# A streaming-encoder layer: the second product's weight loads on another queue, the order of its last products, and the spacing of the attention's softmax blocks

## The chip, the cores and the metric

The kernel runs on one core of a Trainium2 chip, as one program. The metric is the device time of one execution in microseconds (us). The engines are TensorE (PE, with its weight loads as PEld), VectorE (DVE), ScalarE (ACT), GpSimd (POOL) and SyncE (SP, which here only asks for transfers); 16 DMA engines move the data.

## The reference

One pre-norm layer for 1024 positions of width 1024 in float32: a mixing part of three branches with gates, then a SwiGLU feed-forward part, then a final RMSNorm.

```python
proj = rms_norm(x, norm_mix_g) @ w_in          # split into the branches' inputs
o_conv = conv_module(...)                      # GLU, causal depthwise conv of width 31, LayerNorm, SiLU, pointwise product
o_gla = gla(...)                               # 4 heads, chunks of 64
# differential attention: 8 heads, two components of 64, key chunks of 64 up to the query's chunk
s = einsum('bqhtd,bkhtd->bhtqk', q_block, k) * scale
p = softmax(where(mask, s, -inf))
pd = p[:, :, 0] - lam * p[:, :, 1]
o = einsum('bhqk,bkhv->bqhv', pd, v)           # then an RMSNorm
y = sigmoid(m_conv) * o_conv + sigmoid(m_gla) * o_gla + sigmoid(m_diff) * o_diff
x = x + y @ w_out
gate, up = split(rms_norm(x, norm_ffn_g) @ w_ffn_in, 2)   # 2816 each
x = x + (silu(gate) * up) @ w_ffn_out
return rms_norm(x, final_norm_g)
```

## The kernel before

Precision. Every product of float32 matrices is made of three matmuls: the operands are split into a rounded part and the rest (`hilo`: a copy on ACT, L125, and a subtraction on DVE, L126), and `mm3` (L132 to L134) multiplies the parts. A matmul on 512 columns starts 0.23 us after the one before it, where nothing holds it up.

Order. A matmul stream of projections is the main line. Beside it, generators of other work (`spawn`) are stepped by `tick`, a few times in each product; a step of that kind is called a part here. How many ticks lie between a generator's steps is what it yields. The Tile framework adds the waits and may move instructions a little; each engine then executes its list in order, and so does the queue of transfers that SP asks for.

Attention. `diff_core(h)` handles the eight query blocks of one head. Block `qb` has n = 128 (qb + 1) keys. `softmax` multiplies both components' scores (L729, L730), masks the last 64 keys of the upper rows, takes the row maxima (L733 for one component when n is above 512, L736 for both otherwise), and lets ACT take the exponentials (L739). Up to n = 512 both components share one tile of two PSUM banks (`sc`); from the fifth block on (n = 640) each component has a tile of its own. There are two such tiles at a time. `turn` transposes the result, `values` multiplies by the values. The plan (L783 to L785) puts block i's `softmax` at part `at`, its `turn` at `at + LAG[i]` and its `values` three parts after that, and `at` then grows by `SPACE[i]`. While this runs, PE multiplies projections, and DVE also carries the steps of the depthwise convolution (L448). When the cores are done, `conv_norm` and `conv_split` make the operand `u` of the pointwise product.

SwiGLU. Both products are done in Strassen's manner with seven products per group (Winograd's form). The weight operands of the second product are made beforehand from sums, stored to DRAM (`wt_d`, by `right_units`), and loaded back as tiles `tt` of 1 MB by `load_t` (L1288 to L1296), asked for on SP's queue; a ring of 14 tiles is used, so that a load waits until the last product that reads the tile 14 places before it is done. The gated products of the first half are stored to `m_d` (L1231) and come back through `load_mid` (L1324). `load_x3` (L1301) loads the rows that the result is added to.

The last stage goes through 16 `ROUNDS` (t, j0, j1), and each round n through the products p = 0 to 6. The list `order2` (L1349 to L1352) is the order in which the products of two neighbouring rounds alternate. A product adds to one of three chains: `"abacaab"[p]` says which. Chains a and b are the two halves of one two-bank tile `sc`, chain c is a bank `pb`. After each product but the first, DVE adds the chain to the rows x (L1344); the chain's tile is written on by the next product of that chain. In the rounds that finish a row block, `final` takes its square sum on ACT (L1410, L1414), a small step on DVE (L1415), the power -1/2 on POOL (L1416), and the scaling on DVE (L1419); then the result is stored (L1421).

In before, `order2` ends with (15,0), (14,4), (15,1), (15,2), (14,5), (14,6), (15,3), (15,4), (15,6), (15,5). Products of round 14 or 15 have two `k` blocks, six matmuls on 512 columns.

Of the kernel before, what the change touches and what calls it, by code (L numbers as in the profile page):

```python
# [63 lines left out]
AHEAD = 7  # L64

MIX0, MIX1 = 2, 18
LAG = (3, 3, 3, 3, 4, 4, 4, 4)
SPACE = (2, 2, 2, 2, 2, 2, 3, 3)
TAP_RATE = {"head": 0.0, "blocks": 0.45, "gla": 0.45, "diff": 0.82}


def body(nc, tc, I, out):
    x_d, w_d, wf_d, wfup_d, par_d, lq_d, cst_d, msk_d, ffg_d, fng_d = I
    vec, act, pe, pool, sp = nc.vector, nc.scalar, nc.tensor, nc.gpsimd, nc.sync
# [33 lines left out]
    wt_d = dram.tile([(7 * FT // 2 + 1) // 2, P, 4, HALF], F32, name="wt_d")  # L108
# [9 lines left out]
    def f(ap):  # L118
        return ap.bitcast(F32)
# [588 lines left out]
    def diff_core(h):  # L708
# [74 lines left out]
        for i in range(NT):  # L783
            plan += [(at, first, i), (at + LAG[i], second, i), (at + LAG[i] + 3, third, i)]
            at += SPACE[i]  # L785
        now = 0
# [471 lines left out]
    def right_units():  # L1258
        for j in range(PAIRS):
            raw = keep.tile([P, 2, S], F32, tag="kb", name="wo")  # L1260
            for c in range(2):
                sp.dma_start(raw[:, c, :], w_d[first + NU + j, c])
            yield 4
            b11, b12, b21, b22 = (raw[:, c, hs(half)] for c in range(2) for half in range(2))
            ts = fbs[0].tile([P, HALF], F32, tag="ts", name="ts", bufs=1)
            src = (b11, b12, b12, b21, ts, b12, b22)
            for p in range(7):
                if p == 1:
                    vec.tensor_tensor(out=ts, in0=b22, in1=b12, op=ALU.subtract)
                    vec.tensor_tensor(out=b12, in0=b12, in1=b11, op=ALU.subtract)  # L1270
                elif p == 2:
                    vec.tensor_tensor(out=b12, in0=b22, in1=b12, op=ALU.subtract)
                elif p == 5:
                    vec.tensor_tensor(out=b12, in0=b21, in1=b12, op=ALU.subtract)
                u = 7 * j + p
                if u % 2 == 0:
                    to = keep.tile([P, 4, HALF], F32R, tag="kb", name="to")
                hilo(to[:, u % 2 * 2, :], to[:, u % 2 * 2 + 1, :], src[p])
                if u % 2 or u == 7 * PAIRS - 1:
                    n = u % 2 * 2 + 2  # L1280
                    sp.dma_start(wt_d[u // 2][:, 0:n, :], f(to[:, 0:n, :]))
                yield 2
        for i in range(2):
            load_t(i)

    RING = 14
    tt, x3 = {}, {}

    def load_t(i):
        if i >= NTL:  # L1290
            return
        at = i % RING
        pool_, tag = (keep, "kb") if at in (0, 1, 6, 7) else (big, "big") if at < 12 else (fcs["fc"], "tt")
        tt[i] = pool_.tile([P, 4, HALF], F32R, tag=tag, name="tt", bufs=8 if at < 12 else 2)
        n = 2 if i == NTL - 1 and 7 * PAIRS % 2 else 4
        sp.dma_start(f(tt[i][:, 0:n, :]), wt_d[i][:, 0:n, :])  # L1296

    def load_x3(t):
        x = keep.tile([P, 2, D], F32, tag="kb", name="x3")
# [48 lines left out]
    NR = len(ROUNDS)  # L1348
    order2 = [(0, p) for p in range(4)]  # L1349
    for n in range(NR - 1):  # L1350
        order2 += [(n + 1, 0), (n, 4), (n + 1, 1), (n + 1, 2), (n, 5), (n, 6), (n + 1, 3)]
    order2 += [(NR - 1, p) for p in (4, 6, 5)]  # L1352
    makes2 = [(n, p) for n in range(NR) for p in range(7)]
    last_use = {}
    for at, (n, p) in enumerate(order2):
# [11 lines left out]
    for at, (n, p) in enumerate(order):  # L1367
        if at == 4:
            drain()
            tail.release()  # L1370
            fbs.append(tc.alloc_tile_pool(name="fb", bufs=1))
            spawn(t4_block(), 7)
        for _ in range(2 if at > 4 else 1):
            if len(fb.made) < (4 if at < 12 else AHEAD):
                fb.make()
        fb.product(n, p)
        if at == 14:
            spawn(right_units(), 0)
        if n == NU - 1:
            for i in {0: (2, 3), 1: (4, 5), 2: (6, 7), 3: (8, 9), 6: (10, 11)}.get(p, ()):  # L1380
                load_t(i)
            if p == 4:
                load_x3(0)
        if at == len(order) - 12:
            load_mid(0)
        if fb.nxt == len(order):
            load_mid(1)
        if fb.nxt == len(order) and f2.nxt < 7 and len(fb.made) + len(f2.made) < AHEAD:
            f2.make()
        fb.after(n, p)  # L1390
# [32 lines left out]
    for at, (n, p) in enumerate(order2):  # L1423
        for _ in range(2):
            if len(f2.made) < AHEAD:
                f2.make()
        if p == 0 and n in (1, 2):
            load_x3(n + 1)
        if (n, p) == (2, 0):
            for i in (12, 13):  # L1430
                load_t(i)
        if (n, p) == (4, 0):
            sp.dma_start(fng, fng_d)
            act.activation(fng, fng, AF.Copy, scale=ROOT)
        f2.product(n, p)
        f2.after(n, p)
        for i in loads.get(at, ()):
            load_t(i)
# [59 lines left out]
def _program(arrays):  # L1498
    import concourse.bacc as bacc

    nc = bacc.Bacc("TRN2", target_bir_lowering=False, num_devices=1, dynamic_dma_scratch_size=1024)
    ins = [nc.dram_tensor(n, v.shape, mybir.dt.from_np(v.dtype), kind="ExternalInput").ap() for n, v in arrays.items()]
    out = nc.dram_tensor("out_0_dram", (NT, P, D), F32, kind="ExternalOutput").ap()
    with tile.TileContext(nc) as tc:
        body(nc, tc, ins, out)
    return nc
# [9 lines left out]
```

## Time and profile before

| what | value |
| --- | --- |
| median of three runs | 2047.68 us (2047.64 to 2050.73) |
| the profiled execution | 2049.43 us |
| its span | 2047.7 us |
| its granted TensorE clock, mean | 0.999 |
| PE busy | 2009.8 us, 98% |
| DVE, ACT, POOL busy | 72%, 45%, 3% |
| transfers on the hardware queue q1 | 290.19 MB |
| transfers on the software queue q0 | 6.82 MB |

The span is the time from the first to the last record of the profiled execution; the execution's own time is a little longer. In the rows below, a row of a timeline has the start, the duration, the engine, the line, the operation, the tile written from the tiles read, and its form; in brackets stands how long the engine stood idle before it, and what ended that.

### The profile page before, as it was taken

The page shows a single profiled execution, that of the slowest core. Times are in us where ns is not written, and L with a number is a line of the kernel's source. Part 1 is how long each engine was busy: PE and PEld are TensorE (multiplying, and loading weights), DVE is VectorE, ACT ScalarE, POOL GpSimd, SP SyncE. Part 2 cuts the span into 40 slices and gives each one's busy share as a digit, 9 for nine tenths or more (in the row PEclk, how much of TensorE's full clock was granted, in tenths as well). Part 3 has the DMA queues.
Part 4 walks back from the last instruction along what each step waited for, and adds up shares of the span by engine and source line. Part 5 has one row for each costly group of instructions (what it writes and reads, how often), then busy time and mean ns, then how long its engine had stood idle before and what let it go on. Part 6 is the DMA issues. An engine that isn't in the chain of part 4 may idle for free.

```text
span 2047.7 us, 27244 instructions
## 1 busy us (share of the span) xinstructions
PE 2009.8 (98%) x10280; PEld 1693.7 (83%) x10280; DVE 1466.8 (72%) x2306; ACT 930.4 (45%) x1969; POOL 56.6 (3%) x64
## 2 busy tenths in 40 slices
PE   7999999999999999999999999999999999999997
PEld 6888878799999988898988888887888778877775
DVE  7997878577667788787884464459776776656566
ACT  6434434445544455555555461225544544422224
POOL 1000000000000000000000000000000000000000
PEclk9999999999999999999999999999999999999999
DMA  4232242321324443434343555323667666597652
GB/s 158 98 120 88 87 128 98 119 61 58 94 77 124 129 115 81 102 83 116 78 97 99 206 181 166 105 90 112 227 238 253 227 226 237 200 381 270 223 195 88
DMA packets 125124, 298.75 MB, mean 146 GB/s; under 512 B 11744, under 2 KB 56416, under 8 KB 115264
## 3 DMA queue, kind: packets, MB, share of 16 engines
q1 hardware_dynamic: 122256, 290.19, 42.4%
q0 software_dynamic: 2736, 6.82, 2.1%
q8 instruction: 81, 1.33, 0.3%
q14 instruction: 51, 0.42, 0.1%
HBM read 183.19 MB, written 94.90 MB: 136 GB/s over the span
## 4 chain that ended last, share of the span: by engine, by line
PE 72%; issue 13%; DVE 7%; DMA 4%; ACT 3%; POOL 1%; SPq 0%; POOLq 0%; ACTq 0%; DVEq 0%
PE sc L132 12%; PE sc L133 12%; PE sc L134 12%; PE pb L132 11%; PE pb L133 11%; PE pb L134 11%; DVE acc L448 1%; DMA wo<-w_dram 1%; PE pb L766 1%; ACT p L739 1%; DMA wr<-w_dram 1%; DMA wt_d<-to 1%; POOL rs L139 1%; DMA x<-x_d 1%; PE sc L729 1%
## 5 line engine op out<-in xcount | busy, mean ns | idle before, releaser
L448 DVE SCALAR_TENSOR_TENSOR acc<-up,par,acc 128x1024 f32<-128x1024 f32 x240 | 306.8, 1278 | 0.6
L132 PE MATMUL pb<-h,wh 128*128 128x512 f32 x704 | 281.2, 400 | 1.0 <-ACT hf L310 1.0
L134 PE MATMUL pb<-h,wl 128*128 128x512 f32 x704 | 275.9, 392 | 0.0
L133 PE MATMUL pb<-h,wh 128*128 128x512 f32 x704 | 275.6, 391 | 0.0
L125 ACT CAST wh<-wr 128x512 fp32r<-128x512 f32 (+2 forms) x271 | 160.3, 609 | 202.0 <-PE sc L133 90.5
L126 DVE TENSOR_TENSOR wl<-wr,wh 128x512 fp32r<-128x512 f32 (+2 forms) x271 | 180.0, 672 | 61.7 <-ACT wh L125 58.0
L125 ACT CAST wh<-s 128x512 fp32r<-128x512 f32 (+2 forms) x216 | 123.4, 580 | 209.3 <-PE sc L133 144.3
L134 PEld LDWEIGHTS pb<-h,wl 128*128 128x128 f32 x704 | 132.4, 188 | 28.4
L132 PEld LDWEIGHTS pb<-h,wh 128*128 128x128 f32 x704 | 132.9, 189 | 26.1 <-ACT hf L310 1.2
L133 PEld LDWEIGHTS pb<-h,wh 128*128 128x128 f32 x704 | 132.8, 189 | 23.7 <-issue 0.2
L132 PE MATMUL pb<-wh,h 128*128 128x256 f32 x512 | 148.4, 290 | 0.0
L126 DVE TENSOR_TENSOR wl<-s,wh 128x512 fp32r<-128x512 f32 (+2 forms) x216 | 135.4, 638 | 16.4 <-ACT wh L125 16.3
L134 PE MATMUL pb<-wh,h 128*128 128x256 f32 x512 | 144.8, 283 | 0.0
L133 PE MATMUL pb<-wl,h 128*128 128x256 f32 x512 | 144.7, 283 | 0.0
L132 PE MATMUL sc<-bT,wh 128*128 128x512 f32 x352 | 137.4, 391 | 0.7 <-DVE t L1223 0.7
L133 PE MATMUL sc<-bT,wh 128*128 128x512 f32 x352 | 137.0, 389 | 0.0
L134 PE MATMUL sc<-bT,wl 128*128 128x512 f32 x352 | 137.0, 389 | 0.0
L132 PE MATMUL sc<-tt,wh 128*128 128x512 f32 x264 | 106.8, 408 | 7.0 <-DVE x L1344 6.3
L133 PE MATMUL sc<-tt,wh 128*128 128x512 f32 x264 | 103.7, 393 | 0.0
L134 PE MATMUL sc<-tt,wl 128*128 128x512 f32 x264 | 103.0, 393 | 0.0
L132 PE MATMUL sc<-T,wh 128*128 128x512 f32 x256 | 100.0, 391 | 2.0 <-ACT c L986 1.4
L1344 DVE TENSOR_TENSOR x<-x,sc 128x512 f32<-128x512 f32 x80 | 54.6, 686 | 63.6 <-PE sc L134 60.0
(306 smaller groups left out, 4566.7 us busy)
## 6 DMA issues: line engine op xcount, KB each, us to landing
wr<-w_dram SPq DMA_DIRECT2D x146, 512.0 KB, 3.7
wt_d<-to SPq DMA_DIRECT2D x38, 1024.0 KB, 4.2
tt<-wt_d SPq DMA_DIRECT2D x38, 1024.0 KB, 6.1
m_d<-t SPq DMA_DIRECT2D x44, 256.0 KB, 4.2
wo<-w_dram SPq DMA_DIRECT2D x22, 512.0 KB, 5.8
k<-k SPq DMA_DIRECT2D x48, 128.0 KB, 2.8
kl<-kl SPq DMA_DIRECT2D x48, 128.0 KB, 2.4
wr<-m_d SPq DMA_DIRECT2D x12, 384.0 KB, 5.6
```

Source lines behind the costliest of these rows:

```text
L125: a = act.copy(hi, src)
L126: b = vec.tensor_tensor(out=lo, in0=src, in1=f(hi), op=ALU.subtract)
L132: pe.matmul(o, ah, bh, start=start, stop=False, skip_group_check=more)
L133: pe.matmul(o, ah, bl, start=False, stop=False, skip_group_check=more)
L134: pe.matmul(o, al, bh, start=False, stop=stop, skip_group_check=more)
L139: pool.tensor_tensor(out=dst, in0=dst, in1=mhalf[:, 0:width], op=ALU.pow)
L448: op = vec.scalar_tensor_tensor(out=acc, in0=up[:, j:j + S], scalar=w, in1=acc, op0=ALU.mult, op1=ALU.add)
L729: pe.matmul(sc[i][:, c], a["q"][i][:, t], a["k"][i][:, c], start=True, stop=False)
L739: act.activation((p0[:, 0:n], p1)[i], sc[i], AF.Exp, bias=st_[:, i:i + 1], accum_out=st_[:, 2 + i:3 + i])
L766: pe.matmul(ov[:, 0:P], parts[k // 4][:, c], a["v"][:, k, :], start=k == 0, stop=k == nk - 1)
L1344: vec.tensor_tensor(out=x, in0=x, in1=ch["bacaab"[p - 1]], op=ALU.add)
```

## The change

Three edits. The loads of `tt` are asked for by GpSimd (software queue) where SP asked for them (hardware queue). The end of `order2` becomes (15,0), (14,4), (15,1), (15,2), (14,5), (15,4), (14,6), (15,3), (15,5), (15,6). And `LAG` and `SPACE` change: the softmax blocks of a head began at parts 0, 2, 4, 6, 8, 10, 12, 15 and now begin at 0, 2, 4, 6, 9, 11, 13, 16; the transposes were at 3, 5, 7, 9, 12, 14, 16, 19 and are now at 3, 5, 7, 10, 13, 15, 17, 20, and the products with the values three parts after these.

```diff
-LAG = (3, 3, 3, 3, 4, 4, 4, 4)
-SPACE = (2, 2, 2, 2, 2, 2, 3, 3)
+LAG = (3, 3, 3, 4, 4, 4, 4, 4)
+SPACE = (2, 2, 2, 3, 2, 2, 3, 2)
...
         n = 2 if i == NTL - 1 and 7 * PAIRS % 2 else 4
-        sp.dma_start(f(tt[i][:, 0:n, :]), wt_d[i][:, 0:n, :])
+        pool.dma_start(f(tt[i][:, 0:n, :]), wt_d[i][:, 0:n, :])
...
         order2 += [(n + 1, 0), (n, 4), (n + 1, 1), (n + 1, 2), (n, 5), (n, 6), (n + 1, 3)]
-    order2 += [(NR - 1, p) for p in (4, 6, 5)]
+    order2[-2:] = [(NR - 1, 4), (NR - 2, 6), (NR - 1, 3), (NR - 1, 5), (NR - 1, 6)]
```

## Rows read from the trace of the kernel before

**Rows 1.** The page: busy time and share of each engine; chain by engine.
```profile
PE 2009.8 (98%) x10280; PEld 1693.7 (83%) x10280; DVE 1466.8 (72%) x2306; ACT 930.4 (45%) x1969; POOL 56.6 (3%) x64
...
PE 72%; issue 13%; DVE 7%; DMA 4%; ACT 3%; POOL 1%; SPq 0%; POOLq 0%; ACTq 0%; DVEq 0%
```
**Rows 2.** PE's waits: what for, us in total, times, longest.
```profile
PE sc L132 <- DVE x L1344: 6.3, 5, 1.9
PE sc L729 <- ACT p L739: 3.9, 5, 1.0
```
**Rows 3.** Timeline of PE, 805 to 815 us.
```profile
809.82 0.39 PE L133 MATMUL pb<-h,wh 128*128 128x512 f32 x1
811.20 0.44 PE L729 MATMUL sc<-k,q 128*128 128x384 f32 x1 [0.99 <-ACT p L739]
```
**Rows 4.** Timeline of DVE, 804 to 814 us.
```profile
808.44 1.22 DVE L736 TENSOR_REDUCE st<-sc 128x2 f32<-128x1024 f32 x1
```
**Rows 5.** Timeline of PE, 1826 to 1836 us.
```profile
1829.83 0.50 PE L132 MATMUL sc<-tt,wh 128*128 128x512 f32 x1 [1.95 <-DVE x L1344]
```
**Rows 6.** Chain of work that ended last in 1820 to 1836 us: start, us, what.
```profile
1817.14 11.93 DMA x<-x_d
```
**Rows 7.** Stretches: us, busy PE, PEld, DVE, ACT, POOL, clock, DMA share, GB/s.
```profile
1816.00:1827.00 11.00, 11.00 (x48) 8.62 (x47) 5.78 (x13) 2.71 (x7) 0.00 (x0) 1.00 1.02 394
1848.00:2008.00 160.00, 158.26 (x677) 124.30 (x676) 99.39 (x186) 43.25 (x92) 0.00 (x0) 1.00 0.60 211
...
1830.30:1833.70 3.40, 3.40 (x10) 2.62 (x9) 2.72 (x6) 1.80 (x4) 0.00 (x0) 0.50 0.93 329
```
**Rows 8.** Timeline of PE, 1913 to 1919 us.
```profile
1917.59 0.47 PE L132 MATMUL sc<-tt,wh 128*128 128x512 f32 x1 [1.74 <-DVE x L1344]
```
**Rows 9.** Timeline of PE, 2026 to 2040 us.
```profile
2031.67 0.50 PE L132 MATMUL sc<-tt,wh 128*128 128x512 f32 x1 [0.52 <-DVE x L1344]
...
2035.97 0.47 PE L132 MATMUL sc<-tt,wh 128*128 128x512 f32 x1 [1.29 <-DVE x L1344]
...
2038.38 0.50 PE L132 MATMUL sc<-tt,wh 128*128 128x512 f32 x1 [0.78 <-DVE x L1344]
```
**Rows 10.** Line L1296 alone: duration ns, first and last start; landing.
```profile
L1296 SPq DMA_DIRECT2D tt<-wt_d x39: 319/332/927, 1764.8 to 1985.3; - x39
...
DMA to landing us min/median/max: 4.6/6.1/13.2
```
**Rows 11.** SP's waits.
```profile
SPq L1296 <- PE sc L134: 95.6, 26, 8.9
```
**Rows 12.** Line L809 alone, an accumulating store asked for by GpSimd.
```profile
L809 POOL DMA_DIRECT2D y_d<-dgate x12: 862/878/932, 756.1 to 1042.4; - x12
```
**Rows 13.** Timeline of SP, 1964 to 1967 us.
```profile
1965.92 0.33 SPq L1296 DMA_DIRECT2D tt<-wt_d  x1
```
**Rows 14.** Timeline of PE, 1978.7 to 1979 us.
```profile
1978.80 0.39 PE L132 MATMUL sc<-tt,wh 128*128 128x512 f32 x1
```
**Rows 15.** DMA queues in 371.5 to 373.5 us: packets, MB, share.
```profile
q0 software_dynamic: 66, 0.27, 67.5%
q1 hardware_dynamic: 67, 0.27, 36.2%
```
**Rows 16.** Timeline of SP, 1804 to 1832 us.
```profile
1813.89 1.35 SPq L1296 DMA_DIRECT2D tt<-wt_d  x2
```
**Rows 17.** Timeline of DVE, 2027 to 2048 us.
```profile
2033.88 0.75 DVE L1419 SCALAR_TENSOR_TENSOR xn<-x,sm,fng 128x512 f32<-128x512 f32 x1 [0.66 <-POOL sm L1416]
...
2036.90 0.75 DVE L1419 SCALAR_TENSOR_TENSOR xn<-x,sm,fng 128x512 f32<-128x512 f32 x1 [0.66 <-POOL sm L1416]
2037.64 0.69 DVE L1344 TENSOR_TENSOR x<-x,sc 128x512 f32<-128x512 f32 x1
```
**Rows 18.** Timeline of PE, 1198 to 1210 us.
```profile
1202.73 0.39 PE L132 MATMUL pb<-u,wh 128*128 128x512 f32 x1
```
**Rows 19.** Timeline of DVE, 1196 to 1206 us.
```profile
1204.28 1.90 DVE L126 TENSOR_TENSOR u<-c,u 128x512 fp32r<-128x512 f32 x3 [1.00 <-ACT u L125]
```

## What the change does to the time, told before it was known

> **What bounds the kernel now.** I read the page's busy times first: PE is busy 98% of the span, and it carries 72% of the chain that ended last [rows 1]. So time can only go where PE stands still, where its clock is low, or behind its last matmul. The second view is the list of PE's waits [rows 2]: five waits of the second SwiGLU product's matmuls for the DVE addition at L1344, 6.3 us together, and five waits of the score product L729 for the exponential L739, 3.9 us together. The change touches the code around both. The third step is the timeline around each wait.
>
> The score waits all have one place, the fifth query block of a head (five of the eight heads). In the one shown, PE begins the 128x384 product at 811.20 us, 1.38 after the matmul before it, where 0.23 is usual; 0.99 of that is put down to L739 [rows 3]. The block has two score tiles of two banks, and there are two such buffers: its second tile has to wait for both exponentials of the fourth block, and these for the row maximum, which began only at 808.44 and took 1.22, behind the convolution's steps on DVE [rows 4].
>
> The L1344 waits have three places. At 1829.83 PE stood 1.95 us [rows 5], because the addition lacked the residual rows x, a load that took 11.93 us [rows 6] while the DMA engines were full (share 1.02); then TensorE, after standing, ran at half clock (0.50, the 1.2 GHz level) for some 3.4 us [rows 7]. At 1917.59 it stood 1.74 us [rows 8]. Three waits lie in the last rounds, 0.52, 1.29 and 0.78 us [rows 9], where one product follows another into the same two-bank tile and has to wait for the addition that reads it.
>
> **Part 1, the requests on GpSimd's queue.** It moves 39 requests from SP to POOL. It adds no work to PE, DVE or ACT. It takes from SP 39 issues of 0.33 us and 95.6 us of standing for buffers in front of them, 26 times [rows 10, 11]; both lay beside PE's work. On POOL a request of this kind cost 0.88 us where the trace has one [rows 12]; 39 of them are some 34 us on an engine that is 3% busy [rows 1]. What is queued behind a request waiting for its buffer is the next request only; the powers that POOL computes for the last norm come later than the last request at 1985.3 [rows 10]. A late request costs nothing while there is slack: one of the tightest loads is asked for at 1965.92 and its buffer first read at 1978.80, 12.9 us, against 6.1 for a median landing [rows 10, 13, 14], so even 4 us more is hidden; without that slack each late load would cost its lateness on PE.
>
> The open question is what two queues do to SP's other transfers: x, the stored products and their reloads. On one queue x, the second half of which was asked for at 1817.14 [rows 6], stands behind the stores and weight loads asked for before it, the last two of these at 1813.89 [rows 16]. Where the trace has both queues at work, they moved 66 and 67 packets in the same 2 us [rows 15], packet for packet. I apply that to the stretch from 1804 to 1830. The weight packets are the large ones, so they drain early although the small ones of SP are let in between; x is still last of all bytes, and the engines are full until it lands (1.02, 394 GB/s [rows 7]). So I take zero. Gain bound: the 1.95 us and the half clock go, 3.4 x 0.5 = 1.7, together -3.7, and with the 1.74 at 1917.59, -5.4. Loss bound: the stores and reloads slip behind weight packets that were asked for later, +2: the 1.95 us of [rows 5] a second time. Zero is nearest, since the bytes ahead of x are the same.
>
> The Trainium skill ("DMA: Bandwidth & Descriptors", section "Queues, rings and completion order") says that each DMA engine takes turns between queues, changing only at packet boundaries; the 66 and 67 packets agree. By it the sum would carry the same zero here, but the fast side could also be the weights, which is rival B.
>
> **Part 2, the last rounds.** No instruction is added or removed; the last six products change places. A product of the last round is six matmuls, 6 x 0.23 = 1.4 us. Before, (15,4), (15,6) and (15,5) stood in a row on one tile, and (14,5), (14,6) on another. After, (15,4) stands between those two, and (14,6) and (15,3) between (15,4) and (15,5); (15,6) still follows (15,5) directly. An addition takes 0.69, so two of the three waits go and one of about 0.8 stays: PE's last matmul comes 0.52 + 1.29 = 1.8 us earlier, some 2.1 with the restarts [rows 9]. But behind PE stands a chain that runs through DVE, ACT, DVE, POOL and DVE for each of the last four blocks, whose last steps (L1419) stand 3.02 us apart, with an addition of 0.69 in each period [rows 17], and DVE waits in it in order. If that chain sets the end, only an addition that moves out of one period is saved, some 0.6. I take the middle of 0.6 and 2.1, rounded: -1.4. Loss bound: none of it, 0, as no instruction joins.
>
> **Part 3, the softmax blocks.** The numbers give the fifth block one part more behind the fourth, and the sixth to eighth one part later each; the fourth's transposes too. A part is six or nine matmuls of the projection that runs beside it; the inserted one has six, 1.4 us. The longest wait is 0.99, so all five go: 3.9 us by [rows 2], and since the start came 1.15 late where 0.99 was put down, 0.16 more each, together -4.7. The maximum and the exponentials don't move with it, as they were issued before the inserted part. No instruction is added on any engine. What becomes late next: a head ends one part later; the last one passes that to the convolution's norm, and this to the first pointwise product, whose operand was ready just in time: PE took it at 1202.73, the next group of DVE's splits began at 1204.28 after 1.00 us of standing for ACT [rows 18, 19]. A part there is up to 2 us, while two convolution additions leave that stretch; I take +0.3, with 0 and +1.5 as ends. Bounds of the whole part: -5.3 (with another half us of waits in other heads) and +1.5 (no gain, and the late norm paid in full).
>
> **Sum.** 0 - 1.4 - 4.7 + 0.3 = -5.8 us. The profiled execution took 2049.43 us, its span 2047.7 and 1.7 around it; that gives 2043.6. It lay 1.75 above the median of 2047.68; on the median it is **2041.9 us**.
>
> **Rivals.** A: part 1 also clears the wait for x. For it: on one queue x stands behind weights, and off it only behind stores. Against: full engines. Time: 2041.9 - 3.7 = 2038.2. The Trainium skill (same page, section "Issuing engines are not separate DMA queues") says that requests of different engines end on the same 16 DMA engines and save only issue time; by that A could not be, and the time would be the 2041.9.
>
> B, the slower one: the reloads of the stored products lose to weight packets. Each round of the last stage needs a reload of small packets; each of its packets would wait for an 8 KB weight packet asked for later. Place: 1808 to 1990. Price: a wait like that of [rows 5] with its half clock, 1.95 + 1.7 = 3.7 us; it decides from the third one on, 11 - 5.8 = +5: 2053. Against: 39 loads in 220 us leave the engines at a share of 0.60 after 1848 [rows 7], and on one queue the reloads already stood behind whole weight loads.
>
> C: the score wait moves to the next step, since DVE's maximum is late for its own reasons and the sixth block now meets it. Part 3 then gives +0.3 and the time is 2047.68 - 1.1 = 2046.6. For it: DVE's convolution steps go on through the inserted part; against: the sixth block keeps its distance to the fifth.
>
> D: the compiler reorders the end so that part 2 doesn't do what it says: 2043.3. For it: the compiled order of the last products already differs from the written one by a matmul here and there.
>
> **How the numbers follow.** Forecast 0.47, A 0.18, B 0.12, C 0.15, D 0.08. 0.2% is 4.1 us, about what a measurement of this kernel can tell from no change; so faster begins under 2043.6. Faster: A, most of the forecast's own spread (2039.5 to 2044) and half of D: 0.60. Slower: B, 0.12. Same: 0.28. The range for 8 in 10 leaves out B and the lower half of A's spread: 2037.0 to 2048.0.
>
> **What will show it.** The waits of L729 for L739 at the fifth block gone from PE's list, with no new one at the sixth: step 3. Three waits for L1344 left instead of five, one of them in the last rounds, and PE's last matmul some 2 us nearer to the start of the last addition: step 2. Weight loads on the software queue, no DMA among PE's releasers, x landing near 1828, and the half clock still there: step 1. I am wrong if PE waits for pointwise operands near 1203, if x lands early, or if rounds 2 to 13 show new waits on reloads.

## The result: 1% slower, all of it in the last stage

The changed kernel took 2070.44 us (median of four runs, 2067.28 to 2072.73) where the kernel before took 2048.2 in the same comparison: ratio 1.0105, 95% interval 1.0088 to 1.0123. The prediction was 2041.9 us, between 2037.0 and 2048.0. The profiled execution took 2072.73 us, its span 2070.6.

From the page of the changed kernel, busy time of the engines and the queues (packets, MB, share of 16 engines):

```profile
PE 2017.9 (97%) x10280; PEld 1699.6 (82%) x10280; DVE 1465.4 (71%) x2306; ACT 927.6 (45%) x1969; POOL 81.0 (4%) x103
...
q1 hardware_dynamic: 116640, 249.82, 36.9%
q0 software_dynamic: 8352, 47.19, 7.3%
```

The matmuls are the same 10280; 40 MB moved to the software queue, as meant. PE was busy 8.1 us longer with the same matmuls, most of it at half clock: the trace has 20.4 us of half clock between 1829 and 1973 us, where the kernel before has 3.4, and half of the 17.0 us between them is 8.5. The rest of the loss is standing. Lining both traces up by the number of the matmul shows where PE fell behind (times of the changed kernel): it is 1.1 us late at 1790 us, 12.9 late at 1864, 17.3 at 1927, 22.5 at 1993, and no later after that. PE's last matmul is 21.0 us late and the end of the span 22.9, so the last rounds added 1.9.

PE's waits in the changed kernel (us in total, times, longest), to be held against [rows 2]:

```profile
PE sc L132 <- DVE x L1344: 13.1, 8, 4.7
...
PE sc L132 <- ACT pb L958: 3.1, 3, 2.4
PE pb L755 <- DVE dgate L807: 2.2, 3, 0.9
...
PE sc L729 <- DVE p L744: 0.9, 3, 0.4
```

The wait for L739 is gone (part 3 did that), the wait for L1344 doubled. The timeline of PE, cut to the largest of its stops:

```profile
1830.64 0.80 PE L132 MATMUL sc<-tt,wh 128*128 128x512 f32 x1 [4.72 <-DVE x L1344]
1837.74 0.51 PE L132 MATMUL sc<-tt,wh 128*128 128x512 f32 x1 [1.10 <-DVE x L1344]
1849.12 0.50 PE L132 MATMUL sc<-tt,wh 128*128 128x512 f32 x1 [2.39 <-ACT pb L958]
...
1875.94 0.47 PE L132 MATMUL sc<-tt,wh 128*128 128x512 f32 x1 [1.99 <-DVE x L1344]
...
1966.57 0.76 PE L132 MATMUL sc<-tt,wh 128*128 128x512 f32 x1 [3.01 <-DVE x L1344]
```

The first answers to [rows 5]: 4.72 us where there were 1.95. It again has a stretch of half clock (1.2 GHz) behind it, and so has the stop at 1966.57. Stretches of the changed kernel, columns as in [rows 7]:

```profile
1827.00:1834.00 7.00, 3.36 (x8) 2.71 (x9) 0.69 (x1) 0.71 (x2) 1.08 (x2) 0.66 1.00 355
1834.00:1848.00 14.00, 10.97 (x33) 7.47 (x32) 10.20 (x20) 3.33 (x7) 0.00 (x0) 0.80 0.97 368
...
1966.50:1969.50 3.00, 2.93 (x7) 2.38 (x8) 1.93 (x4) 0.00 (x0) 0.00 (x0) 0.50 1.02 431
```

Two things are to be explained: 1800 to 1850 us, and the single stops up to 1970.

**What DVE does at the later stops.** DVE in the changed kernel near the stop of 3.01 us; L901 is a sum of products that were stored and reloaded (`wr`, `mr`), from which a left operand is made:

```profile
1960.64 0.55 DVE L901 TENSOR_TENSOR s<-mr,s 128x384 f32<-128x384 f32 x1
1965.27 0.56 DVE L901 TENSOR_TENSOR s<-wr 128x384 f32<-128x384 f32 x1 [4.08 <-DMA wr<-m_d]
1965.75 0.68 DVE L1344 TENSOR_TENSOR x<-x,sc 128x512 f32<-128x512 f32 x1
```

And the same place of the kernel before:

```profile
1944.00 0.56 DVE L901 TENSOR_TENSOR s<-mr,s 128x384 f32<-128x384 f32 x1
1946.05 0.69 DVE L1344 TENSOR_TENSOR x<-x,sc 128x512 f32<-128x512 f32 x1 [1.49 <-PE sc L134]
...
1948.18 0.55 DVE L901 TENSOR_TENSOR s<-wr 128x384 f32<-128x384 f32 x1
```

In the changed kernel the sum waits for its reload, and the addition that PE waits for stands behind it. The compiled order shows that this is no accident of timing. DVE's instructions there, S n.1 being the first sum of round n, X n.p the addition after product p, l the low parts of operands:

```
before:  ... X8.5 l10.1 S10.6 X8.6 l10.2 X9.3 l10.3 S11.1 S11.2 X9.4 ...
changed: ... X8.5 l10.1 S10.6 S11.1 X8.6 l10.2 X9.3 l10.3 S11.2 X9.4 ...
```

S5.1, S7.1 and S11.1 had moved ahead of X2.6, X4.6 and X8.6; S9.1 and S13.1 stood so before as well, and the stop of [rows 8] is that of S9.1. In the first rounds, X1.1 and X1.2, which need the late rows x, now stood ahead of X0.5 and X0.6. None of that is in the diff. PE's products of the first rounds, a few matmuls and copies of ACT near these places, and SP's requests stand in another order too. Why is not shown; presumably the framework orders each engine's list by when it takes the operands to be ready, and takes a reload to land sooner when no weights stand before it in SP's list.

### The profile page after: what moved, and what is told of

Read it like the earlier page. It is cut to its first block, busy times and chain, and to the rows that moved or that the text cites. A ratio compares the mean times of both kernels' runs of the same rounds, so it can differ in the third digit from the quotient of the medians.

```text
span 2070.6 us, 27304 instructions
## 1 busy us (share of the span) xinstructions
PE 2017.9 (97%) x10280; PEld 1699.6 (82%) x10280; DVE 1465.4 (71%) x2306; ACT 927.6 (45%) x1969; POOL 81.0 (4%) x103
## 5 line engine op out<-in xcount | busy, mean ns | idle before, releaser
L132 PE MATMUL sc<-tt,wh 128*128 128x512 f32 x264 | 109.6, 418 | 17.8 <-DVE x L1344 13.1
L1344 DVE TENSOR_TENSOR x<-x,sc 128x512 f32<-128x512 f32 x80 | 54.7, 685 | 75.8 <-PE sc L134 63.4
L133 PE MATMUL sc<-tt,wh 128*128 128x512 f32 x264 | 106.7, 404 | 0.0
```

What stands on the lines that cost most here:

```text
L132: pe.matmul(o, ah, bh, start=start, stop=False, skip_group_check=more)
L133: pe.matmul(o, ah, bl, start=False, stop=False, skip_group_check=more)
L1344: vec.tensor_tensor(out=x, in0=x, in1=ch["bacaab"[p - 1]], op=ALU.add)
```

## The experiments

Times are medians beside runs of the kernel before on the same chip, whose own median lay between 2047.9 and 2049.6; so the ratio counts. The runs are called e1 to e17, and the expectations, each written before its run, stand in the order in which the labels are then named. In the kernels with order edges the lines below L901 are two further down (L1344 is L1346). An order edge says which of two instructions of one engine comes first in its list; it adds no wait.

**Each part alone, and all but part 1.** The edits are the diff's own (e1 to e4).

> Part 1 alone: the weight loads on GpSimd's queue, the other two parts as before. Changed against before: 2070.4 to 2048.2, +22.2 us. Theory Q (part 1 is the cause): 2070 to 2074, PE in the last stage falling behind by 12 us between 1790 and 1864 us and by another 9 to 10 us up to 1993 us, as in the changed kernel. Rival O2 (the new order of the last products, or the attention's spacing, shifts the order that the compiler makes): 2048 to 2052.

> Part 2 alone. My step in the prediction: -1.4 us (2046.8), between -2.1 and -0.6. Rival: the last chains are held by the two buffers xn, which come free only when a finished block has been stored, and the new order finishes two first halves later; then the end comes up to 2 us later although PE is done sooner: 2048 to 2050.

> Part 3 alone. My step in the prediction: -4.4 us (2043.8). The trace of the changed kernel shows the five waits of L729 for L739 gone, but others in their places (PE waiting for DVE at L807 and L681), and PE only about 1 us ahead at 1170 us: by that -0.5 to -1.5, 2046.7 to 2047.7.

> Parts 2 and 3 without part 1 (the weight loads stay on SP's queue). Theory Q: the whole loss is gone, 2045 to 2048.5, no wait of PE over 2.5 us between 1800 and 2000 us. Rival O2: 2066 to 2072, as in the changed kernel.

Part 1 alone: 2070.46, ratio 1.0104 (1.009 to 1.0118). Part 2: 1.000 (0.9991 to 1.0009). Part 3: 1.0002 (0.9993 to 1.001). Parts 2 and 3 together: 1.0003 (0.9994 to 1.0012). Theory Q holds: part 1 is the whole loss, and its compiled order on DVE in the last stage is that of the changed kernel up to the last rounds. My step of -4.4 us for part 3 falls, as its interval ends at -1.4. The -1.4 of part 2 lies inside its interval (-1.8 to +1.8); no gain is seen, but so small a one is not ruled out.

**Order or transfers.** Part 1 with edges on DVE alone (e5, e6), and the kernel before with such edges (e7, e8):

```diff
+    for n in range(5, 15, 2):                 # e5, e6, e8: sums behind additions
+        behind(sums[n][1], adds[n - 3, 6])
...
+    behind(adds[1, 1], adds[1, 3])            # e6 also, with products (0,4),(1,1),(0,5),(1,3),(0,6),(1,2)
+    behind(adds[1, 1], adds[0, 6])
+    behind(sums[2][1], adds[1, 1])
...
+    for n, p in ((5, 3), (7, 4), (11, 3)):    # e7: the other way round, on the single queue
+        behind(adds[n - 3, 6], sums[n][1])
+        behind(adds[n - 2, p], adds[n - 3, 6])
```

> Part 1, and in addition an order edge on DVE only (no wait): in the odd rounds n = 5 to 13 the first sum (L901) of the reloaded products is queued behind the addition (n - 3, 6), as the compiler had it before in three of the five places. The weight loads stay on GpSimd's queue. Theory H (what costs is the sum's wait for its reload standing ahead of the addition that PE needs): the stops near 1874, 1903, 1933 and 1966 us are gone, 9 to 11 us less than part 1 alone. Theory C (the two queues make the transfers late, whatever the order): within 2 us of part 1 alone.

> As the run before, and also the first rounds in the order that the kernel before had: products (0,4), (1,1), (0,5), (1,3), (0,6), (1,2), with addition (1,1), which needs the late rows x, behind (0,6) and (1,3), and the first sum of round 2 behind (1,1). The queues are those of part 1. Theory H: 2046 to 2052, nearly all of the loss back. Theory C: 2064 or more.

> The kernel before with its single queue, and the order of the changed kernel forced in three places: the first sums of rounds 5, 7 and 11 ahead of the additions (2,6), (4,6) and (8,6). Theory H: three new stops of PE of 2 to 4 us, with or without a stretch of half clock behind them: +5 to +10 us, 2053 to 2058. Theory C: no change, 2047 to 2049.

> The kernel before with its single queue, and the sums of the odd rounds 5 to 13 behind the additions (n - 3, 6). Before had rounds 9 and 13 the other way. Theory H: the stop of 1.7 to 1.9 us at 1917 us goes, 2045.5 to 2046.8. Theory C: no change, 2047.5 to 2049.

e5: 2059.13 (ratio 1.0055, 1.0039 to 1.007), 10 to 11 us less than part 1 alone; between 1860 and 2000 us PE has no stop left that the timeline names. Some 1.7 us of this is the stop of S9.1, which the kernel before had too [rows 8] and which these edges also remove. e7: 2056.86 (1.0044, 1.003 to 1.0057), 7.8 slower with edges on DVE alone. It is not the clean reverse of e5, though: with these edges the compiled lists of PE and ACT changed at the three places as well. DVE and, in the second fence, PE of e7 at the second of the forced places (S7.1):

```profile
1889.27 0.56 DVE L126 TENSOR_TENSOR wl<-s,wh 128x384 fp32r<-128x384 f32 x1 [0.61 <-ACT wh L125]
...
1890.22 0.55 DVE L901 TENSOR_TENSOR s<-wr 128x384 f32<-128x384 f32 x1
1890.68 1.27 DVE L1346 TENSOR_TENSOR x<-x,sc 128x512 f32<-128x512 f32 x2
```

```profile
1891.51 0.47 PE L132 MATMUL sc<-tt,wh 128*128 128x512 f32 x1 [2.64 <-DVE x L1346]
```

Only this one costs much, 2.64 us and the half clock behind it; at the others PE stands less than 1 us. DVE did not stand for a reload before the sum here: the addition is late because the sum and four splits, which waited for ACT, had moved ahead of it. So e7 shows that another order alone costs time, not that this wait for a reload does; that rests on e5 and on the changed kernel's rows above. e8: 2048.09, 0.9998 (0.9989 to 1.0006): its trace has no stop near 1917, as theory H said, but the time is that of theory C, no change; its interval reaches down to -2.3 us, so a gain of the size of that stop is not ruled out either. e6 is a miss: 2061.78 (1.0072), 2.6 more than e5. Its compiled first rounds came near those of the kernel before but were not the same. This order does not give the loss back; at the same place PE then stood for the reloads. Something in the transfers themselves had to be left.

**Which loads, and why (e9, e10, e12).**

```diff
-        sp.dma_start(f(tt[i][:, 0:n, :]), wt_d[i][:, 0:n, :])
+        (pool if i < RING else sp).dma_start(...)      # e9;  e10: (sp if i < RING else pool)
...
+        for j in range(n):                             # e12
+            pool.dma_start(f(tt[i][:, j, :]), wt_d[i][:, j, :])
```

> Only the first 14 weight loads (those asked for up to 1832 us) on GpSimd's queue, the other 25 on SP's; the sums of the odd rounds behind the additions. The run with all loads on GpSimd's queue and these sums took 2059.1, +10, all of it between 1790 and 1864 us. Theory C1 (what is left of the loss comes from the two queues at work together while the DMA engines are full): 2057 to 2061, the same. Theory L (it comes from the later loads): 2047 to 2050.

> The other half: loads 14 to 38 on GpSimd's queue, the first 14 on SP's, the same sums edges. Theory C1: 2046 to 2049, as the kernel before; the stop at the rows x of some 2 us stays and no other is above 1.5 us. Theory L: 2057 to 2061.

> All weight loads on GpSimd's queue, each asked for in four parts, so that its packets are 2 KB and no longer 8 KB; the same sums edges. Theory P (the DMA engines take packets of the two queues in turn, so that every small packet of SP's stores and reloads stands behind a large weight packet): the store asked for near 1808 us lands in 8 to 13 us and not in 17, and the time is 3 to 8 us under the 2059.1 of the run with 8 KB packets. Theory R (what costs is the order in which SP now asks, the rows x ahead of the last store): within 2 us of 2059.1.

e9: 2060.45 (1.0069). e10: 2047.99 (1.0004, 0.9993 to 1.0015). The 14 loads asked for up to 1832 us carry the rest; the 25 later ones cost nothing on GpSimd's queue once the sums stand right. e12 is a miss in its time, 2068.39 (1.0101), although the share went as theory P says. Its weight packets are 4 KB in the trace, not the 2 KB expected; those of the changed kernel are 8 KB. Both queues from 1816 to 1822 us, first the changed kernel, then e12:

```profile
q0 software_dynamic: 299, 2.18, 86.4%
q1 hardware_dynamic: 343, 0.30, 14.6%
```

```profile
q0 software_dynamic: 486, 1.57, 65.5%
q1 hardware_dynamic: 643, 0.82, 37.1%
```

SP's queue moved 0.82 MB and not 0.30. But the weights, in smaller pieces, were then under way up to 1835 us, the store still stood in SP's queue behind the rows x, and it landed after 15.2 us. So the smaller packet alone was no cure.

**SP's order, and relief (e13, e15, e17).** SP's requests in the changed kernel, and two of its transfers with their landing times in us (rows x asked for at 1808.98 and a store asked for at 1809.49; before, the same two took 7.4 and 10.5):

```profile
1812.57 4.12 SPq L1301 DMA_DIRECT2D x<-x_d  x2
1816.88 0.37 SPq L1231 DMA_DIRECT2D m_d<-t  x1
1817.35 7.12 SPq L1301 DMA_DIRECT2D x<-x_d  x2
1830.59 0.90 SPq L1324 DMA_DIRECT2D mr<-m_d  x2
```

```profile
x<-x_d SPq DMA_DIRECT2D x1, 512.0 KB, 9.4
m_d<-t SPq DMA_DIRECT2D x1, 256.0 KB, 17.1
```

Without the weights, SP asks for 1 MB of rows x ahead of the last store and for 2 MB ahead of the reload `mr`. The reload is asked for when the last store has landed: before, at 1826.69, and here at 1830.59.

```diff
+    for i in range(2):                                  # e13, on top of e6: SP's old order
+        behind(asked["x", 1, i], asked["m"])
+        behind(asked["x", 2, i], asked["r", 2, 1])
+        behind(asked["x", 3, i], asked["r", 3, 1])
...
+    gate = pool.tensor_copy(out=sm[:, 31:32], in_=x3[5][:, 0:1])    # e15, on top of e5
+    held = [load_t(i) for i in range(8, 12)]                        # ... and each behind gate
...
+            gate = pool.tensor_copy(out=sm[:, 31:32], in_=mid[3][3][:, 0, 0:1])   # e17, on top of e13
+            held = [load_t(i) for i in (12, 13)]                                  # ... and each behind gate
```

> All weight loads on GpSimd's queue, the sums edges and the first rounds' order as in the run of 2061.8 us, and also SP's requests in the order of the kernel before: x of round 1 behind the last store, x of round 2 behind the reload of round 2, x of round 3 behind that of round 3 (order edges on SP, no waits). Theory R (SP's order is what costs): 2050 to 2054, the reload of round 2 landing near 1831 us. Theory C (full DMA engines, shared with GpSimd's queue): 2058 or more.

> All weight loads on GpSimd's queue and the sums edges (2059.1 us so far), but loads 8 to 11, first read after 1839 us and landing by 1826, are asked for only when the rows x of round 1 have landed: a copy of one column of x on GpSimd stands in front of them. This takes 4 MB out of the stretch from 1806 to 1826 us. Theory C: x and the last store land 5 us earlier or more, the stop at x shrinks from 5 us to under 1, 2049 to 2053. Theory R: 2057 to 2060.

> The run of 2057.7 us with weight loads 12 and 13 alone held back until the reload of round 3 has landed (a copy of one column of it on GpSimd stands in front of them); every order on DVE is the same. Theory C (weights on the other queue, asked for beside the reload, take its share of the DMA engines): the reload of round 3 lands by 1837 us, 7 to 8 us from its request where it took 12 to 13, the stop of 5.4 us near 1840 us shrinks to under 2, and the time is 2050 to 2054. Theory R: no change, 2056 to 2059.

e13: 2057.74 (1.0037, 1.0024 to 1.0051), 4 us less than e6 by the medians and 7 by the ratios, with the lists of PE and DVE the same: SP's order is a part, not all. Against e5 it is only 1 to 4 us less, as e6 itself took 2.6 more than e5. e17, which in addition holds back two loads: 2052.42 (1.0018, 1.0008 to 1.0028), another 4 to 5 less. The reload of round 3 in e13 and in e17 (KB, us to landing; the kernel before has 7.5):

```profile
wr<-m_d SPq DMA_DIRECT2D x2, 384.0 KB, 12.6
```

```profile
wr<-m_d SPq DMA_DIRECT2D x2, 384.0 KB, 7.5
```

PE's stop of 5.24 us at 1844.09 in e13 is gone in e17, with the order of every engine's other work unchanged. e15 is a miss, 2064.21 (1.0072), outside both ranges; but its trace shows theory C's mechanism best. Up to 1822 us it is relieved: the last store landed after 4.3 us and x after 7.3. Then its gate opened, and six weight loads were asked for within 3.3 us, just as SP asked for the reloads. The two queues of e15 from 1826 to 1842 us; the chain that ended last there; and PE:

```profile
q0 software_dynamic: 787, 5.79, 87.3%
q1 hardware_dynamic: 789, 0.78, 14.2%
```

```profile
1822.89 19.66 DMA mr<-m_d
```

```profile
1845.04 0.79 PE L132 MATMUL sc<-tt,wh 128*128 128x512 f32 x1 [14.75 <-DVE x L1346]
```

Nearly packet for packet, 787 to 789 (707 to 759 without those of 4 bytes), but 5.79 MB to 0.78, as the packets are of 8 KB on one queue and 1 KB on the other: a reload of 384 KB, 4.4 us in the kernel before, took 19.7, and PE stood for 14.75.

**The end, and a better version (e11, e14, e16).**

```diff
-            xn = norm[t] = fc.tile([P, D], F32, tag="xn", name="xn", bufs=2)
+            xn = norm[t] = fc.tile([P, D], F32, tag="mr" if t in (3, 7) else "xn", name="xn", bufs=2)   # e11, e16
...
+    load_mid(2)                     # e14, e16: loads 8 to 11 asked for here, with the sums edges
+    load_x3(1)
+    for i in range(8, 12):
+        load_t(i)
```

> Part 2 (the new order of the last products), with the last two blocks' results in the two buffers of the reloads (tag mr), which are free by then, so that four blocks have a buffer. Part 2 alone was equal to before (ratio 1.000). Theory X (its gain on PE, 1.1 us, is lost to the first half of the last blocks, which waits for a stored block's buffer): the last scaling starts some 2 us nearer to PE's last matmul, 2046.5 to 2048 where before gives 2049. Rival: the chain through DVE, ACT and POOL is as long anyway, 2048.5 to 2050.

> The single queue of before, the sums edges, and loads 8 to 11 asked for behind x of round 1 and the reload of round 2 in the program. Theory C, used the other way: the stop of 2 us at x and the half clock behind it go, 2043.5 to 2046 where before gives 2048 to 2049. Against it: the compiler changes other places with this order; then 2047 to 2051.

> The run before and parts 2 and 3 with four buffers for the last results. Parts 2 and 3 gave nothing by themselves (ratios 1.000): if that is so here as well, within 1 us of the run before; if all pieces add up, 2 us less than it.

In part 2 alone the last first halves (L1410 on ACT, L1411 on DVE) come late:

```profile
2041.67 0.61 ACT L1410 ACTIVATE xn<-x 128x512 f32<-128x512 f32 x1
```

```profile
2042.41 0.69 DVE L1411 TENSOR_TENSOR xn<-x,fng 128x512 f32<-128x512 f32 x1 [0.61 <-ACT xn L1410]
...
2043.90 0.75 DVE L1419 SCALAR_TENSOR_TENSOR xn<-x,sm,fng 128x512 f32<-128x512 f32 x1 [0.67 <-POOL sm L1416]
```

The store that frees the buffer landed at 2041.37, while ACT was still at the step before, L1418. With four buffers (e11) the last L1419 begins 4.0 us after the start of PE's last matmul, where part 2 alone has 5.4 and before 3.4. The trace moves as theory X says; the time does not and lies where the rival had it: 2049.16, 1.0007 (0.9999 to 1.0016). e14 is a miss: 2049.32, 1.0001 (0.9992 to 1.001); its stop at x is 0.97 us and not 1.95, but others came. e16, all pieces on the single queue: 2047.81 against 2049.56, ratio 0.999 (0.9981 to 1.0), not clear of no change. No version beats the kernel before by more than its measurement can tell.

## Why the prediction was wrong, point by point

- **Part 1, taken as zero with a loss bound of 2 us: this step failed, at 21.** Three of its sentences were wrong. "It adds no work to PE, DVE or ACT" is true and was no answer: moving the requests alone (e1) changed the compiled order, and with it sums on DVE moved ahead of additions that PE needs: 10 to 11 us (e5), of which the kernel before had some 1.7 already. That it works through assumed landing times is argued; the order is shown. "Both lay beside PE's work", of SP's 95.6 us of standing [rows 11], left out what that standing did: it held SP's later requests back, behind the weights and in a good order. Freed of it, SP asked for x early, and the last store and its reload came 4 us late: 4 to 7 us of time, measured in the first rounds' order of e6 (e6 to e13). "The bytes ahead of x are the same" held for x, which landed at 1829.78 where [rows 6] give 1829.07, but not for the stores and reloads, which the sum had only in its loss bound.
- **Rival B named one of the mechanisms** (packets of the reloads against weight packets) at a chance of 0.12, with 3.7 us a wait. For two of the loads it is shown, 4 to 5 us (e13 to e17). Its stretch, 1808 to 1990, was too long: e9 and e10 put all that is not the order on DVE before 1850. How that half divides among packets, SP's order and the order of the first rounds is not settled. The rows 66 to 67 packets [rows 15] were read rightly; I drew from them that the weights drain early, and not that what is small pays for it: 17.1 us for a store, 12.6 for a reload, 19.7 in e15. The Trainium skill ("DMA: Bandwidth & Descriptors", section "Queues, rings and completion order") has each DMA engine take turns between queues, changing only at packet boundaries; the 787 to 789 packets of e15 agree.
- **Rival A** (x lands early) did not happen. The Trainium skill ("DMA: Bandwidth & Descriptors", section "Issuing engines are not separate DMA queues") has requests of several engines save only issue time. The prediction took that as neither gain nor loss; part 1 alone measured 1.0104, and the measurement decides: the order of the requests and of the engines' lists changed with the queue.
- **The slack of the weights** was right: PE's list of the changed kernel has no wait for them, and the tightest three landed some 7 us ahead of their first use.
- **Part 2, -1.4: measured 0, give or take 1.8.** Not two of the three waits went on PE but one, that of 1.29 (in e2, 0.54 and 0.87 stayed), and its last matmul came 1.1 us earlier where 1.8 to 2.1 were said. The end did not follow it: the last L1419 came later behind it. The term that was missing is, by the traces, the ring of two xn buffers: [rows 17] show the chain, and I counted its steps but not what its first step waits for. That this ring costs time is not shown, as e11 gained none.
- **Part 3, -4.4: measured 0, -1.4 to +2.** The waits for L739 went. In their places PE waits for L807 (2.2 us in three), for L744 (0.9 in three, before 0.4 in one) and in two places for other steps of DVE: 4.6 us of standing between 600 and 1200 us where before has 4.3. PE still gains some 1.2 us there, by the line-up of both traces, and the median shows none of it. Rival C had half of that: the wait moves because DVE is late, but most of it moved to L807, not to the scores. So the step that failed took the five waits as gained in full, with nothing but the norm late in exchange.
- **The range** left out what it had itself listed as unknown, and its own sign of being wrong, new waits on reloads in rounds 2 to 13, came. With B at 0.12 and no case for the compiler's order but at the end (D), 2048.0 was too low an upper bound.

## What to carry to other kernels

Moving a request to another queue changes three things: what the old queue asks for next, what it shares the DMA engines with, and the order in which a scheduling compiler lays out every engine's list; look at the compiled orders first. Here two queues shared by packets, so keep bulk loads on the queue of the small, urgent transfers that they must not overtake, or hold them back until those have landed. A wait that vanishes from PE's list is a gain only if the engine that was late has less to do.

## What the runs showed of the hardware that was not expected

A request of 1 MB cost GpSimd 0.54 us (median of 39), not the 0.88 of an accumulating store [rows 12]. Two queues in full use moved 787 and 789 packets in 16 us, at 5.79 and 0.78 MB. No run has the weights on a second hardware queue, so whether it matters that theirs was the software one stays open. With the sums, the first rounds, SP's order and two loads put back, but not the queue, 1.0018 was left (e17), of which the trace shows one stop of 4.3 us, for the reload of round 2, whose store landed 1.3 us later than before. The compiled order of the first rounds in e17 was still not quite that of the kernel before, so this rest is not settled.
